# Four query tiles as one Strassen-like set, and a new order of the attention's fillers

## Chip, cores and metric

One core of one Trainium2 chip runs the whole layer. The metric is the device time of the program in microseconds, the median of several runs. All inputs are float32. The engines' short names are those of the profile: PE (TensorE), PEld (its weight loads), DVE (VectorE), ACT (ScalarE), POOL (GpSimd), SP (SyncE, which issues most loads).

## The reference

One decoder layer on 512 tokens of 1024 features. The normalised input `h` goes through one wide projection; the part that matters here is the local branch, with 16 query heads of 64 on 4 key heads:

```python
proj = h @ w_in[i]
qk_ml, v_ml, o_ml, if_pre, q_sw, k_sw, v_sw, g_a, g_b = jnp.split(proj, split_idx, axis=-1)
...
y_b = swa_with_sinks(q_sw.reshape(B, S, SW_Q_HEADS, SW_HEAD_DIM), k_sw..., v_sw..., sinks[i])
merged = jax.nn.sigmoid(g_a) * (y_a @ w_branch_a[i]) + jax.nn.sigmoid(g_b) * (y_b @ w_branch_b[i])
```

Attention is causal with a window of 128 tokens, so a block of 128 queries sees its own and the previous block of keys. The other branch is a chunkwise mLSTM; its queries and keys (`qk_ml`) pass a short convolution and a SiLU. Behind both come the gates, an output projection, an MLP, a gated embedding and a last norm.

## The kernel before

**Products.** Every float32 matrix is split into a high part (a cast on ACT, `wh`) and a low part (a subtraction on DVE, `wl`), and a product is three matmuls per block of 128: high by high, low by high, high by low. `load_w` (L242) makes the parts, four buffers of each deep. `proj_T` (L552) computes one tile, 128 output features for all 512 tokens, in 24 matmuls of 512 columns.

**Sets of seven.** `seven` (L646) multiplies a 2x2 block matrix by another with seven half products instead of eight. One factor is `h`, halved by tokens and by parity of its feature blocks; its parts A11, A12, A22 and its sums S1 to S4 are formed once and kept. The other is a weight in four quarters b11 to b22, which DVE sums in place (four sums of 128x1024). Three PSUM accumulators are used: X (tag `a`, one tile over two banks), Y (tag `t`) and Z (tag `g`). In order: p1 = A11 b11 on X, c11 from A12 b21 on Y, u2 on X with S2, p5 = S1 b11 on Z, c22 with S3 b12 on X, c12 with S4 b22 on Z, c21 with A22 b21 on X. `post` copies p1, u2 and p5 out on ACT and adds them to c11, c12 and c22 on DVE.

`gate_proj` (L837) uses this for the two gate projections: per call two sets of four tiles, each product 24 matmuls of 256 columns (two tiles by four feature blocks by three). Its weights come by `quads` (L264), four loads of 512 KB on SP's queue.

**Queries.** `q_proj` (L617) computes one of eight query tiles with `proj_T` and splits each of its two head halves: ACT casts 64 rows (`qs`), DVE subtracts the rest into the other 64. Tile 0 is made early, tiles 1 to 3 behind the gate projections (L896), tiles 4 to 7 as fillers.

**Attention.** 16 units (two key pairs, four blocks of 128 tokens, two heads). `swa_probs` (L921) is the first part of a unit: eight matmuls (kk, kl), the mask, the maximum, the exponentials on ACT with their sums, the scaling. It runs two units ahead (LOOK). After every fourth unit `swa_out` transposes the probabilities of two blocks and multiplies them by the values (half-array matmuls into `pst`, whose results are `yb`). The key pair 0 reads query tiles 0 to 3, the pair 1 tiles 4 to 7. Ahead of some units one **filler** is called, a projection that the attention doesn't wait for: query tiles 4 to 7 and seven of the eight mLSTM query and key tiles (`qk_proj`, with four more operations for the convolution, `acc`). The eighth stands behind the attention. Eleven slots have a filler:

```python
fill = [lambda: qk_proj(0)] + [lambda i=i: q_proj(i) for i in range(4, 8)]
fill += [lambda i=i: qk_proj(i) for i in (4, 1, 5, 2, 6, 3)]
for u in range(16):
    if u % 3 or u < 3:
        fill.pop(0)()
```

**Order.** Outside the first stage the order on each engine is worked out ahead of time by the framework, from the data's dependences, the buffers and the order of the text as priority; on the chip each engine then runs its instructions in that fixed order. All instructions are issued by one helper, so the trace shows L109 for nearly all of them, and rows are told apart by tiles: `psg<-h,wh` is a filler's or query tile's matmul (`proj_T`), `psa<-hS,wh` and `psg<-hS,wh` are products with the sums of `h`, `psa<-kk,qs` and `psa<-kl,qs` are a unit's logits, `lm` its probabilities.

Of the kernel before, what the change touches and what calls it, by code (L numbers as in the profile page):

```python
# [12 lines left out]
AF = mybir.ActivationFunctionType  # L13
# [104 lines left out]
def block_kernel(  # L118
# [6 lines left out]
    w_o: bass.AP,  # L125
    w_vsif: bass.AP,
    w_qsw: bass.AP,
    w_ksw: bass.AP,
    w_ga: bass.AP,
    w_gb: bass.AP,  # L130
# [51 lines left out]
    def ps_a():  # L182
        return pp.tile([P, 1024], F32, tag="a", bufs=2, name=nm("psa"))
# [9 lines left out]
    def act_r(n="r"):  # L193
        return ap.tile([P, 512], F32R, tag="act", bufs=NACT, name=nm(n))
# [59 lines left out]
    def pairs(a, b):  # L254

        return [(a[0], b[0]), (a[0], b[1]), (a[1], b[0])]
# [295 lines left out]
    def proj_T(wd, i, bank=ps_g):  # L552
        ps = bank()
        mm_T(ps, load_w(wd[i], KT * P, KT), hT)
        return ps
# [58 lines left out]

    qs = {}

    def q_proj(i):  # L617
        ps = proj_T(w_qsw, i)
        for ab in range(2):
            s, o = HALF[ab], HALF[1 - ab]  # L620
            t = act_r("qs")
            A.copy(t[s, :], ps[s, :])
            V.tensor_sub(t[o, :], ps[s, :], r32(t[s, :]))
            qs[i, ab] = t

    q_proj(0)

# [15 lines left out]

    ADDED = {"c11": "p1", "c22": "p5", "c12": "u2"}

    def seven(form, prod, X, Y, Z, b, post, own_first=False, sums_late=False):  # L646

        b11, b12, b21, b22 = b  # L650
        n = range(len(b11))
        for i in n:
            prod(X, A11, form(b11[i]), i, True)
        post("p1", X)

        def weight_sums():
            for i in n:
                V.tensor_sub(b12[i], b22[i], b12[i])
                V.tensor_add(b11[i], b12[i], b11[i])

        if sums_late:
            w21 = [form(t) for t in b21]
            with tc.issue_after(last_low[0].ins):
                weight_sums()
        else:
            weight_sums()
        for i in n:
            prod(Y, A12, w21[i] if sums_late else form(b21[i]), i, True, True)
        own = last_mm[0].ins
        if own_first:  # L670
            with tc.issue_after(last_low[0].ins):
                late_sums()
        post("c11", Y)
        for i in n:
            w = form(b11[i]) if sums_late else None
            with tc.issue_after(last_low[0].ins) if sums_late else ExitStack():
                V.tensor_sub(b21[i], b21[i], b11[i])
            w = w or form(b11[i])
            with tc.issue_after(own) if own_first else ExitStack():
                prod(X, S2, w, i, False)  # L680
            V.tensor_sub(b11[i], b22[i], b11[i])
        post("u2", X)
        for i in n:
            prod(Z, S1, form(b11[i]), i, True)
        post("p5", Z)
        for i in n:
            prod(X, S3, form(b12[i]), i, False)
        post("c22", X)
        for i in n:
            prod(Z, S4, form(b22[i]), i, False, True)  # L690
        post("c12", Z)
        for i in n:
            prod(X, A22, form(b21[i]), i, False, True)
        post("c21", X)


    vm = []
# [124 lines left out]
    def gate_columns():  # L822
# [11 lines left out]
            V.tensor_copy(gc[:, t * NT : t * NT + t + 1, :], pgc[:, t * NT * 4 : (t * NT + t + 1) * 4].rearrange("p (a b) -> p a b", b=4))  # L834
        V.tensor_copy(gc[:, NT * NT :, :], pgc[:, NT * NT * 4 : (NT * NT + NT) * 4].rearrange("p (a b) -> p a b", b=4))

    def gate_proj(wd, beside={}):  # L837

        out_d = [None] * 4
        for j in range(2):  # L840
            raws = quads(wd[4 * j : 4 * j + 4], ["wr"] * 4 if j == 0 else ["pT"] * 2 + ["wr"] * 2)
            X = ps_a().rearrange("p (n c) -> p n c", n=2)[:, :, :256]
            Y, Z = [[new()[:, :256] for _ in range(2)] for new in (ps_t, ps_g)]
            keep = {}
            res = [sp.tile([P, 2, 512], F32, tag="lm", bufs=LMB, name=nm("gr")) for _ in range(2)]

            def prod(ps, f, w, _, first, last=False):
                for t in range(2):
                    ops = []
                    for k in range(4):  # L850
                        ops += pairs([h[:, k, t * P : (t + 1) * P] for h in w], f[k])
                    chain(ps[:, t, :] if ps is X else ps[t], ops, first, last, True)

            def both(op, o, ps, *k):
                if ps is X:
                    op(o, ps, *k)
                else:
                    for t in range(2):
                        op(o[:, t, :], ps[t], *[a[:, t, :] for a in k])

            def post(what, ps):
                if what[0] != "c":
                    keep[what] = act_f(what).rearrange("p (n c) -> p n c", n=2)
                    both(A.copy, keep[what], ps)
                else:
                    half, nh = int(what[1]), int(what[2]) - 1
                    o = res[nh][:, :, 256:] if half == 1 else res[nh][:, :, :256]
                    if what in ADDED:
                        k = keep[ADDED[what]]
                        both(V.tensor_add, k, ps, k)  # L870
                        ps = k
                    A.activation(o, ps, AF.Sigmoid)
                for work in beside.pop((j, what), ()):
                    work()

            seven(lambda r: load_w(None, 1024, 4, r), prod, X, Y, Z, [raws[i : i + 1] for i in range(4)], post)
            for nh in range(2):
                d = dp.tile([P, 2, 512], F32, name=nm("gd"))
                nc.gpsimd.dma_start(out=d, in_=res[nh])
                out_d[2 * nh + j] = d  # L880
        return out_d

    loaded = {}

# [4 lines left out]
            nc.sync.dma_start(out=loaded[0], in_=put[i // 2])  # L889
        return loaded[0][:, i % 2, :]  # L890

    gbd = gate_proj(w_gb, {(0, "p5"): [gates], (1, "c11"): [gate_columns]})
    gad = gate_proj(w_ga)

    for i in range(1, 4):
        q_proj(i)  # L896


    qk = [None] * 8
# [106 lines left out]
    for n in (3, 2, 1):  # L1006
        V.tensor_sub(vd[n], vs[n], vs[n - 1])

    fill = [lambda: qk_proj(0)] + [lambda i=i: q_proj(i) for i in range(4, 8)]
    fill += [lambda i=i: qk_proj(i) for i in (4, 1, 5, 2, 6, 3)]  # L1010
    for u in range(LOOK):
        swa_probs(*units[u])
    for u in range(16):
        if u % 3 or u < 3:
            fill.pop(0)()
        if u + LOOK < 16:
            swa_probs(*units[u + LOOK])
        if u % 4 == 3:
            kp, n, _ = units[u]
            swa_out(kp, (n - 1, n))  # L1020
# [915 lines left out]


_ORDER = [
    "x", "p", "w_qkml", "w_vml", "w_o", "w_vsif", "w_qsw", "w_ksw", "w_ga", "w_gb", "w_a", "w_b", "w_out",
    "w_up", "w_upb", "w_down", "w_pg", "w_pp", "pw", "g_mix", "g_ml", "g_mlp", "g_ple", "g_fin", "conv", "b_if", "sinks",  # L1940
]

# [15 lines left out]
def _halves(w):  # L1958


    return w.reshape(4, 2, P, 2, 2, 256).transpose(4, 1, 3, 2, 0, 5).reshape(8, P, 1024)


def _by_set(w):
# [25 lines left out]
def _layout(i):  # L1990
    w = i["w_in"][0]
    down = i["w_down"][0]
    return {
        "x": i["x"][0],
        "p": i["p"][0, 0].T.reshape(2, P, S).transpose(1, 0, 2).reshape(P, 2 * S),
        "w_qkml": _t_form(w[:, 0:1024]),
        "w_vml": _by_quarter(w[:, 1024:2048]),
        "w_o": _by_quarter(w[:, 2048:3072]),
        "w_vsif": _tok_form(np.concatenate([w[:, 4360:4616], w[:, 3072:3080]], axis=1), KT, 264)[0],
        "w_qsw": _t_form(_heads(w[:, 3080:4104])),  # L2000
        "w_ksw": _t_form(w[:, 4104:4360]),
        "w_ga": _halves(w[:, 4616:5640]),
        "w_gb": _halves(w[:, 5640:6664]),
        "w_a": _t_form(i["w_branch_a"][0]),
        "w_b": _t_form(_heads(i["w_branch_b"][0].T).T),
        "w_out": _by_quarter(i["w_out"][0]),
        "w_up": _t_form(i["w_up"][0][:, :1024]),
        "w_upb": _by_set(i["w_up"][0][:, 1024:]),
        "w_down": np.concatenate([_quarters(down[q * 1024 : (q + 1) * 1024]) for q in range(4)], axis=0),
        "w_pg": _tok_form(i["w_ple_gate"][0], 2, 512),  # L2010
        "w_pp": _tok_form(i["w_ple_proj"][0], 2, 512),
        "pw": np.stack([np.concatenate([i["p"][0, 0].T[o : o + P], i["w_ple_proj"][0][o : o + P, :512]], axis=1) for o in (0, P)]),
        "g_mix": i["norm_mix_g"],
        "g_ml": _columns(i["mlstm_norm_g"][0]),
        "g_mlp": _columns(i["norm_mlp_g"][0]),
        "g_ple": _columns(i["norm_ple_g"][0]),
        "g_fin": i["final_norm_g"][None, :],
        "conv": i["conv_qk"][0].reshape(4, KT, P).transpose(2, 1, 0).reshape(P, KT * 4),
        "b_if": i["b_if"],
        "sinks": i["sinks"],  # L2020
    }
# [19 lines left out]
```

## Time and profile before

| | us |
|---|---|
| median of 3 runs | 862.68 (861.21 to 863.85) |
| the profiled execution | 861.12 |
| its span, first to last instruction | 858.9 |
| PE busy | 849.8 (99%) |
| DVE busy | 712.8 (83%) |
| ACT busy | 526.0 (61%) |
| POOL busy | 59.4 (7%) |

The profiled execution is 2.2 us longer than its span, and 1.56 us shorter than the median. The span falls into the stage of `h` and the first projections (to 122 us), the gate projections (to 204), three query tiles (to 221), the attention (to some 326), the mLSTM and the merge (to 443), and the output projection, the MLP and the rest. PE runs at a granted clock of 0.998 on average. Matmul records overlap one another, and their ends are modelled: the time from one start to the next is the pitch, which the chain of work that ended last shows best, as its pieces lie end to end.

### The profile page before, as it was taken

To read this page: it belongs to the slowest core of one execution; us is meant where nothing else is said; L and a number is where in the kernel's file an instruction comes from. 1 tells how busy PE (TensorE), PEld (TensorE's weight loads), DVE (VectorE), ACT (ScalarE), POOL (GpSimd) and SP (SyncE) were. 2 spreads that over 40 slices of the span, in tenths; PEclk is the share of its full clock that TensorE was granted. 3 is DMA by queue.
4 is the path that set the end of the run, shared out by engine and by line. 5 is a ranking of instruction groups with operands and counts; after the bars stand their busy time and mean duration, and the time that the engine had idled before them with its cause. 6 is when DMAs were issued, how large, how long until landed. Compare 5 with 4: busy or idle time off the path is not lost.

```text
span 858.9 us, 12796 instructions
## 1 busy us (share of the span) xinstructions
PE 849.8 (99%) x4864; PEld 737.9 (86%) x4864; DVE 712.8 (83%) x1039; ACT 526.0 (61%) x907; POOL 59.4 (7%) x92
## 2 busy tenths in 40 slices
PE   9999999999999999999999999999999999999996
PEld 8888789999877878888888888899889989988886
DVE  6998978774698899767897799879988997899657
ACT  7786657554577677863343586458628744774743
POOL 2221111000000000000020000000000000010000
PEclk9999999999999999999999999999999999999999
DMA  8777235436121256565224381743355364634402
GB/s 291 225 206 263 98 124 202 162 129 220 50 98 36 89 177 239 196 245 189 107 52 131 104 228 47 214 134 121 85 186 147 108 172 135 173 102 130 140 1 98
DMA packets 37535, 125.70 MB, mean 146 GB/s; under 512 B 5213, under 2 KB 5213, under 8 KB 37474
## 3 DMA queue, kind: packets, MB, share of 16 engines
q1 hardware_dynamic: 28146, 95.77, 32.2%
q0 software_dynamic: 9184, 28.85, 13.9%
q8 instruction: 38, 0.62, 0.3%
q14 instruction: 23, 0.19, 0.1%
q10 hardware_dynamic: 144, 0.26, 0.1%
HBM read 106.51 MB, written 11.54 MB: 137 GB/s over the span
## 4 chain that ended last, share of the span: by engine, by line
PE 86%; issue 6%; DVE 4%; ACT 2%; DMA 1%; POOL 0%; POOLq 0%; ACTq 0%; DVEq 0%
PE psp L109 34%; PE psg L109 34%; PE psa L109 13%; PE pst L109 5%; ACT lm L109 1%; DVE wl L109 1%; DMA wo<-in_w_out 1%; ACT wh L109 0%; DMA wh<-in_w_b 0%; DVE wr L109 0%; DVE ya L109 0%; DVE lm L109 0%; DVE mx L109 0%; ACT jk L109 0%; DVE wq L109 0%
## 5 line engine op out<-in xcount | busy, mean ns | idle before, releaser
L109 ACT CAST wh<-wr 128x1024 fp32r<-128x1024 f32 (+1 forms) x148 | 153.7, 1049 | 146.4 <-DVE wr L109 52.2
L109 DVE TENSOR_TENSOR wl<-wr,wh 128x1024 fp32r<-128x1024 f32 (+1 forms) x157 | 189.4, 1213 | 56.5 <-ACT wh L109 49.0
L109 PE MATMUL psp<-x,wh 128*128 128x256 f32 x672 | 121.3, 283 | 0.0
L109 PE MATMUL psp<-wh,uf 128*128 128x512 f32 x336 | 106.3, 390 | 0.0
L109 PEld LDWEIGHTS psp<-x,wh 128*128 128x128 f32 x672 | 105.0, 192 | 0.3
L109 PE MATMUL psp<-x,wl 128*128 128x256 f32 x336 | 95.1, 283 | 0.0
L109 PE MATMUL psg<-h,wh 128*128 128x512 f32 x256 | 80.1, 393 | 0.0
L109 PEld LDWEIGHTS psp<-wh,uf 128*128 128x128 f32 x336 | 63.1, 188 | 14.3 <-issue 1.2
L109 ACT CAST wh<-wd 128x1024 fp32r<-128x1024 f32 x45 | 47.2, 1049 | 33.0 <-PE psp L109 27.8
L109 PE MATMUL psp<-wl,uf 128*128 128x512 f32 x168 | 65.5, 390 | 0.0
L109 PEld LDWEIGHTS psp<-x,wl 128*128 128x128 f32 x336 | 64.5, 192 | 0.0
L109 DVE TENSOR_TENSOR wl<-wd,wh 128x1024 fp32r<-128x1024 f32 x45 | 54.7, 1218 | 3.2 <-ACT wh L109 3.2
L109 PEld LDWEIGHTS psg<-h,wh 128*128 128x128 f32 x256 | 46.9, 188 | 8.9
L109 PE MATMUL psg<-h,wl 128*128 128x512 f32 x128 | 50.0, 391 | 0.0
L109 DVE TENSOR_TENSOR uf<-F,uf 128x512 fp32r<-128x512 f32 (+3 forms) x36 | 35.0, 983 | 6.4 <-ACT uf L109 6.4
L109 PE MATMUL psg<-yb,wh 128*128 128x512 f32 x128 | 40.1, 393 | 0.0
L109 PE MATMUL psg<-x,wh 128*128 128x512 f32 x128 | 39.5, 390 | 0.0
L109 DVE TENSOR_TENSOR wr<-wr,wr 128x1024 f32<-128x1024 f32 x31 | 37.9, 1222 | 1.4 <-DMA wr<-in_w_gb 0.5
L109 PEld LDWEIGHTS psp<-wl,uf 128*128 128x128 f32 x168 | 31.5, 188 | 6.7 <-DVE wl L109 0.3
L109 PE MATMUL psg<-wh,uf 128*128 128x512 f32 x112 | 36.5, 389 | 0.0
L109 ACT CAST uf<-F 128x512 fp32r<-128x512 f32 (+3 forms) x36 | 30.7, 856 | 7.5 <-DVE F L109 7.1
L109 PE MATMUL psg<-ya,wh 128*128 128x512 f32 x112 | 34.8, 391 | 0.0
(348 smaller groups left out, 2033.3 us busy)
## 6 DMA issues: line engine op xcount, KB each, us to landing
wr<-in_w_down SPq DMA_DIRECT2D x16, 512.0 KB, 4.1
wd<-in_w_down SPq DMA_DIRECT2D x16, 512.0 KB, 4.3
wr<-in_w_upb SPq DMA_DIRECT2D x12, 512.0 KB, 4.0
wd<-in_w_upb SPq DMA_DIRECT2D x12, 512.0 KB, 4.4
wr<-in_w_qsw SPq DMA_DIRECT2D x8, 512.0 KB, 4.4
gd<-gr POOLq DMA_DIRECT2D x8, 512.0 KB, 3.3
wr<-in_w_qkml SPq DMA_DIRECT2D x8, 512.0 KB, 3.2
wr<-in_w_b SPq DMA_DIRECT2D x8, 512.0 KB, 3.6
```

The lines of the kernel that those rows point to most:

```text
L109: ins = op(*args, **kw)
```

## The change

Query tiles 1 to 4 are no longer four `q_proj` calls (three behind the gate projections, one filler) but one set of seven half products, `q_set`, behind the gate projections, on the kept S1 to S4. The body of `gate_proj` becomes `by_features`, which both use. In the set of queries the order inside `seven` is **swapped**: the S3 product follows the S2 product on X and is copied out (u3), then S1 on Z gives c22 with u3 added, then c21 on X, and c12 last. A result of the set is 256 tokens of two tiles; `put_q` splits it in pieces of 64x256. The fillers are ten: three query tiles and seven of the mLSTM's, in other slots and another order. The weights of the eight query tiles lie in two arrays now.

```diff
+    def put_q(i, c0, n, ps):
         for ab in range(2):
             s, o = HALF[ab], HALF[1 - ab]
-            t = act_r("qs")
+            if (i, ab) not in qs:
+                qs[i, ab] = act_r("qs")
+            t = qs[i, ab][:, c0 : c0 + n]
             A.copy(t[s, :], ps[s, :])
             V.tensor_sub(t[o, :], ps[s, :], r32(t[s, :]))
-            qs[i, ab] = t
+
+    def q_proj(i):
+        put_q(i, 0, S, proj_T(w_qsw, i - 4 if i else 0))
...
         post("u2", X)
+        if swapped:
+            for i in n:
+                prod(X, S3, form(b12[i]), i, False)
+            post("u3", X)
         for i in n:
             prod(Z, S1, form(b11[i]), i, True)
-        post("p5", Z)
-        for i in n:
-            prod(X, S3, form(b12[i]), i, False)
-        post("c22", X)
-        for i in n:
-            prod(Z, S4, form(b22[i]), i, False, True)
-        post("c12", Z)
-        for i in n:
-            prod(X, A22, form(b21[i]), i, False, True)
-        post("c21", X)
+        if swapped:
+            post("c22", Z)
+        else:
+            post("p5", Z)
+            for i in n:
+                prod(X, S3, form(b12[i]), i, False)
+            post("c22", X)
+        rest = [("c12", Z, S4, b22), ("c21", X, A22, b21)]
+        for what, ps, f, b in rest[::-1] if swapped else rest:
+            for i in n:
+                prod(ps, f, form(b[i]), i, False, True)
+            post(what, ps)
...
+    def q_set():
+
+        def done(half, nh, ps):
+            for t in range(2):
+                put_q(1 + 2 * nh + t, 256 if half == 1 else 0, 256, ps[:, t, :])
+
+        by_features(w_qset, ["wr"] * 4, done, swapped=True)
...
-    for i in range(1, 4):
-        q_proj(i)
+    q_set()
...
-    fill = [lambda: qk_proj(0)] + [lambda i=i: q_proj(i) for i in range(4, 8)]
-    fill += [lambda i=i: qk_proj(i) for i in (4, 1, 5, 2, 6, 3)]
+    fill = [lambda: q_proj(7), lambda: qk_proj(6), lambda: q_proj(6), lambda: q_proj(5), lambda: qk_proj(4), lambda: qk_proj(2), lambda: qk_proj(1), lambda: qk_proj(5), lambda: qk_proj(0), lambda: qk_proj(3)]
...
-        if u % 3 or u < 3:
+        if u in (0, 2, 3, 5, 6, 10, 11, 13, 14, 15):
```

## Rows read from the trace of the kernel before

**Rows 1.** The page, busy time of TensorE (share) and its instructions.

```profile
PE 849.8 (99%) x4864; PEld 737.9 (86%) x4864; DVE 712.8 (83%) x1039; ACT 526.0 (61%) x907; POOL 59.4 (7%) x92
```

**Rows 2.** Windows: stretch, its length, each engine's busy time, clock, DMA share, GB/s.

```profile
164.00:204.40 40.40, 40.40 (x338) 40.40 (x337) 28.88 (x31) 22.60 (x31) 2.67 (x5) 1.00 0.44 157
204.40:220.60 16.20, 16.20 (x73) 13.38 (x73) 6.43 (x7) 5.79 (x9) 0.53 (x1) 1.00 0.58 195
220.60:326.20 105.60, 105.42 (x550) 81.36 (x549) 91.35 (x198) 75.56 (x239) 2.14 (x4) 1.00 0.29 98
```

**Rows 3.** Chain that ended last: start us, us, what, instructions.

```profile
21.52 0.87 PE psa L109 x8
...
161.19 5.76 PE psa L109 x48
166.95 2.88 PE pst L109 x24
...
204.39 16.35 PE psg L109 x72
...
276.53 3.58 PE pst L109 x16
```

**Rows 4.** Groups by form, PE, the attention: form, count, busy us, mean ns, idle.

```profile
L109 PE MATMUL psg<-h,wh 128*128 128x512 f32 x193 | 60.8, 394 | 0.0
L109 PE MATMUL psg<-h,wl 128*128 128x512 f32 x97 | 38.0, 392 | 0.0
L109 PE MATMUL psa<-kk,qs 128*128 128x256 f32 x64 | 16.5, 291 | 0.0
...
L109 PE MATMUL psa<-ident,lm 128*128 128x128 f32 x64 | 8.3, 275 | 0.1
L109 PE MATMUL pst<-lm,vs 128*64 128x512 f32 x32 | 7.9, 592 | 0.0
...
L109 PE MATMUL psg<-yb,wh 128*128 128x512 f32 x8 | 2.6, 405 | 0.0
```

**Rows 5.** Groups by form, DVE, the whole span.

```profile
L109 DVE TENSOR_TENSOR wl<-wr,wh 128x1024 fp32r<-128x1024 f32 x154 | 186.9, 1220 | 56.5 <-ACT wh L109 49.0 <-DMA wh<-in_w_b 5.1 <-PE psp L109 2.2
...
L109 DVE TENSOR_TENSOR qs<-psg,qs 64x512 fp32r<-64x512 f32 x16 | 11.0, 688 | 3.3 <-ACT qs L109 2.9
```

**Rows 6.** Timeline, DVE: start us, us, instruction, idle before and its releaser.

```profile
189.25 0.42 DVE L109 TENSOR_TENSOR p<-pst,p 128x256 f32<-128x256 f32 x1
```

**Rows 7.** The page, DMA issues: count, KB each, us to landing.

```profile
wr<-in_w_qsw SPq DMA_DIRECT2D x8, 512.0 KB, 4.4
```

**Rows 8.** Timeline, PE and ACT, around the copy of u2 in `w_ga`'s second set.

```profile
192.70 0.40 PE L109 MATMUL psg<-hS,wh 128*128 128x256 f32 x2
192.78 1.05 ACT L109 CAST wh<-wr 128x1024 fp32r<-128x1024 f32 x1 [1.25 <-PE psa L109]
193.73 0.58 ACT L109 COPY u<-psa 128x512 f32<-128x512 f32 x1
```

**Rows 9.** Timeline, PE, at the attention's start.

```profile
223.39 0.39 PE L109 MATMUL psg<-h,wh 128*128 128x512 f32 x1
223.66 0.39 PE L109 MATMUL psa<-kk,qs 128*128 128x256 f32 x1
223.89 0.28 PE L109 MATMUL psa<-kl,qs 128*128 128x256 f32 x1
224.00 0.40 PE L109 MATMUL psg<-h,wh 128*128 128x512 f32 x1
```

**Rows 10.** Timeline, output projection: a copy out of the bank that PE goes on with.

```profile
442.75 1.09 ACT L109 COPY q<-psg 128x512 f32<-128x512 f32 x2
...
443.38 0.50 PE L109 MATMUL psg<-wh,mg 128*128 128x512 f32 x1 [0.22 <-ACT q L109]
```

**Rows 11.** Timeline, PE and DVE: first and last instruction of one unit's first part.

```profile
287.28 0.28 PE L109 MATMUL psa<-kk,qs 128*128 128x256 f32 x1
...
295.41 0.69 DVE L109 TENSOR_TENSOR lm<-lm,rc 128x512 f32<-128x512 f32 x1
```

More of the change, by code (lines that the diff above doesn't have):

```diff
@@ L127, in block_kernel @@
     w_qsw: bass.AP,
+    w_qset: bass.AP,
     w_ksw: bass.AP,
@@ L615, in block_kernel @@
     qs = {}
-    def q_proj(i):
-        ps = proj_T(w_qsw, i)
+    def put_q(i, c0, n, ps):
         for ab in range(2):
             s, o = HALF[ab], HALF[1 - ab]
-            t = act_r("qs")
+            if (i, ab) not in qs:
+                qs[i, ab] = act_r("qs")
+            t = qs[i, ab][:, c0 : c0 + n]
             A.copy(t[s, :], ps[s, :])
             V.tensor_sub(t[o, :], ps[s, :], r32(t[s, :]))
-            qs[i, ab] = t
+    def q_proj(i):
+        put_q(i, 0, S, proj_T(w_qsw, i - 4 if i else 0))
     q_proj(0)
@@ L644, in block_kernel, with seven @@
     ADDED = {"c11": "p1", "c22": "p5", "c12": "u2"}
-    def seven(form, prod, X, Y, Z, b, post, own_first=False, sums_late=False):
+    def seven(form, prod, X, Y, Z, b, post, own_first=False, sums_late=False, swapped=False):
         b11, b12, b21, b22 = b
@@ L835, in gate_columns, with by_features, prod, both @@
         V.tensor_copy(gc[:, NT * NT :, :], pgc[:, NT * NT * 4 : (NT * NT + NT) * 4].rearrange("p (a b) -> p a b", b=4))
+    def by_features(blocks, tags, done, beside={}, swapped=False):
+        added = dict(ADDED, c22="u3") if swapped else ADDED
+        raws = quads(blocks, tags)
+        X = ps_a().rearrange("p (n c) -> p n c", n=2)[:, :, :256]
+        Y, Z = [[new()[:, :256] for _ in range(2)] for new in (ps_t, ps_g)]
+        keep = {}
+        def prod(ps, f, w, _, first, last=False):
+            for t in range(2):
+                ops = []
+                for k in range(4):
+                    ops += pairs([h[:, k, t * P : (t + 1) * P] for h in w], f[k])
+                chain(ps[:, t, :] if ps is X else ps[t], ops, first, last, True)
+        def both(op, o, ps, *k):
+            if ps is X:
+                op(o, ps, *k)
+            else:
+                for t in range(2):
+                    op(o[:, t, :], ps[t], *[a[:, t, :] for a in k])
+        def post(what, ps):
+            if what[0] != "c":
+                keep[what] = act_f(what).rearrange("p (n c) -> p n c", n=2)
+                both(A.copy, keep[what], ps)
+            else:
+                if what in added:
+                    k = keep[added[what]]
+                    both(V.tensor_add, k, ps, k)
+                    ps = k
+                done(int(what[1]), int(what[2]) - 1, ps)
+            for work in beside.pop(what, ()):
+                work()
+        seven(lambda r: load_w(None, 1024, 4, r), prod, X, Y, Z, [raws[i : i + 1] for i in range(4)], post, swapped=swapped)
     def gate_proj(wd, beside={}):
@@ L840, in gate_proj @@
         for j in range(2):
[L841 to L844, printed above, removed]
             res = [sp.tile([P, 2, 512], F32, tag="lm", bufs=LMB, name=nm("gr")) for _ in range(2)]
[L847 to L876, printed above, removed]
+            def done(half, nh, ps):
+                A.activation(res[nh][:, :, 256:] if half == 1 else res[nh][:, :, :256], ps, AF.Sigmoid)
+            by_features(wd[4 * j : 4 * j + 4], ["wr"] * 4 if j == 0 else ["pT"] * 2 + ["wr"] * 2, done, beside.get(j, {}))
             for nh in range(2):
@@ L881, in gate_proj, with done @@
         return out_d
+    def q_set():
+        def done(half, nh, ps):
+            for t in range(2):
+                put_q(1 + 2 * nh + t, 256 if half == 1 else 0, 256, ps[:, t, :])
+        by_features(w_qset, ["wr"] * 4, done, swapped=True)
     loaded = {}
@@ L890, in gate_of @@
         return loaded[0][:, i % 2, :]
-    gbd = gate_proj(w_gb, {(0, "p5"): [gates], (1, "c11"): [gate_columns]})
+    gbd = gate_proj(w_gb, {0: {"p5": [gates]}, 1: {"c11": [gate_columns]}})
     gad = gate_proj(w_ga)
-    for i in range(1, 4):
-        q_proj(i)
+    q_set()
     qk = [None] * 8
@@ L1938 @@
 _ORDER = [
-    "x", "p", "w_qkml", "w_vml", "w_o", "w_vsif", "w_qsw", "w_ksw", "w_ga", "w_gb", "w_a", "w_b", "w_out",
+    "x", "p", "w_qkml", "w_vml", "w_o", "w_vsif", "w_qsw", "w_qset", "w_ksw", "w_ga", "w_gb", "w_a", "w_b", "w_out",
     "w_up", "w_upb", "w_down", "w_pg", "w_pp", "pw", "g_mix", "g_ml", "g_mlp", "g_ple", "g_fin", "conv", "b_if", "sinks",
@@ L1961, in _halves, with _one_set @@
     return w.reshape(4, 2, P, 2, 2, 256).transpose(4, 1, 3, 2, 0, 5).reshape(8, P, 1024)
+def _one_set(w):
+    return w.reshape(4, 2, P, 2, 256).transpose(1, 3, 2, 0, 4).reshape(4, P, 1024)
 def _by_set(w):
@@ L1992, in _layout @@
     down = i["w_down"][0]
+    q_sw = _heads(w[:, 3080:4104])
     return {
@@ L1999, in _layout @@
         "w_vsif": _tok_form(np.concatenate([w[:, 4360:4616], w[:, 3072:3080]], axis=1), KT, 264)[0],
-        "w_qsw": _t_form(_heads(w[:, 3080:4104])),
+        "w_qsw": np.concatenate([_t_form(q_sw[:, :P]), _t_form(q_sw[:, 5 * P :])], axis=0),
+        "w_qset": _one_set(q_sw[:, P : 5 * P]),
         "w_ksw": _t_form(w[:, 4104:4360]),
```

## The prediction

> **What bounds the kernel now.** I read the page first. TensorE (PE) is busy for 99% of the span [rows 1]. A reader should not stop there: matmul records overlap and their ends are modelled, so a busy PE can still be waiting. The second view, busy time by stretch, has to say where another engine could be behind it [rows 2]. In the gate stage (164.0 to 204.4 us) PE and its weight loads fill everything while VectorE (DVE) has 28.88 of 40.40 us. In the three query tiles behind it DVE has 6.43 of 16.20. In the attention (220.6 to 326.2) it has 91.35 of 105.60, so there it is close behind PE. The clock column stands at 1.00 in all of them, the upper level of 2.4 GHz; the change leaves no gap long enough to give a reason for another level.
>
> The third view, the chain that ended last, gives the pitch of the matmuls, because its pieces lie end to end [rows 3]. A product of 24 matmuls with 256 columns takes 2.88 us, 120 ns each. Seventy-two with 512 columns take 16.35 us, 227 ns each, so one query tile (24 of them) costs 5.45 us. Eight transposes take 0.87 us, 109 ns each. Sixteen half-array products take 3.58 us, 224 ns each.
>
> With these pitches I add up the attention's PE work from its counts [rows 4]: 193 + 97 filler matmuls at 227 ns are 65.8 us; 64 kk and as many kl at 120 ns, 15.4; 64 transposes, 7.0; 56 half-array products (32 of lm, the others of pT), 12.5; and 12 first matmuls of the next stage, 2.7. That is 103.4 us in a stretch of 105.6. So **PE is the bound in the attention too**, and only some 2.2 us are waits, in pieces of about a tenth of a microsecond. A change here earns what it takes from PE's work, and loses what it adds in waits.
>
> **The change, part by part.**
>
> *Query tiles one to four.* Removed: 4 x 5.45 = 21.80 us of PE. Added: seven products of the gate stage's kind, 7 x 2.88 = 20.16 us. **PE saves 1.64 us.** The work also moves: before, three tiles (16.35 us) stood ahead of the attention and four were fillers; now 20.16 us stand ahead of it and three are fillers. The attention thus starts 3.8 us later and holds 5.45 us less PE work.
>
> The Trainium skill, page "TensorE: Matmul & The Clock Gate", section "Back-to-back issue gap", gives 262 cycles for 256 columns and 518 for 512. At 2.4 GHz that would be an estimate of 109 and 216 ns, and a saving of 2.4 us instead of 1.64. The chain's pieces show 120 and 227 ns, so I keep 1.64.
>
> *DVE.* Removed for four tiles: a low part of 1.22 us and two query subtractions of 0.69 us each [rows 5], 4 x 2.60 = 10.4 us. Added: seven low parts and four weight sums, 11 x 1.22 = 13.4 us; three additions in two pieces of 128x256 at 0.42 [rows 6], 2.5 us; sixteen subtractions of 64x256. Such a subtraction is not in the trace. Half of the 64x512 one would be 0.34, the 128x256 addition is 0.42; I take 0.42, the row with the same number of columns, 6.7 us. Together 22.7, **12.3 us more on DVE**. It is paid at nothing for the most part: DVE has 11.5 + 9.8 us idle in the two stretches ahead of the attention [rows 2], and the low parts are made some products ahead. What spills is the last post (two additions, four subtractions, 2.5 us). The attention's DVE work becomes 91.35 - 2.6 + 2.5 = 91.2 us in about 100.2, a share of 0.91 where it was 0.87. The cover gets thinner; it is not gone. ScalarE gains three more casts (3 x 1.05) and smaller copies, in stretches where it has 18 us idle of 40 [rows 2]; I cost that at nothing.
>
> *Loads.* Four 512 KB loads in the place of four; half a megabyte lands in 4.4 us [rows 7]. The last two wait on SP's queue for buffers that the second gate pass gives back, as the second gate projection's loads wait for the first's. At that seam the chain runs without a break: the 48 matmuls from 161.19, two products with the seam between them, take 5.76 us, and the next product 2.88 [rows 3]. Only later weight loads queue behind them on SP. Nothing.
>
> *The swapped order.* Here a wait is added. Before, the S1 product stood between the S2 and the S3 product on bank X, and hid the copy of u2. Now S3 follows S2 on X and must wait for that copy. What is queued behind it is all of PE. The second gate projection shows the copy's time: the next product begins at 192.70, the copy of u2 starts at 193.73, behind a weight cast on ScalarE, and takes 0.58 [rows 8]. If PE stood still until then, it would lose 194.31 - 192.70 = 1.6 us. That is the upper bound. The lower is a switch between products: where the order slips single kk, kl pairs between filler matmuls, the pitch from kk to kl is 0.23 instead of 0.12 us [rows 9], 0.1 for a switch and 0.2 for there and back. The order is worked out ahead by the framework from its own estimates, and these rows show that it fills a foreseen wait with other ready matmuls; the S1 product is ready there. Where nothing else was allowed, in the output projection, PE did stand: its next matmul was let go by the copy q at 443.38, idle for 0.22 us in the record [rows 10]. I take **+0.4**, near the filling rows. The later swap (c21 ahead of c12) has one product between every copy and its reuse, so nothing there.
>
> The Trainium skill, "Perfetto Trace Analysis", section "Optimizing Tensor Performance" (Matmuls), advises rotating independent matmul groups through different banks, so that one's evacuation overlaps the next one's matmuls. S3 right behind S2 on X breaks that rule. What it costs by the rows is the 1.6 us above, and that is the second rival below.
>
> *The attention's start.* c21 completes the queries for the first two blocks one product ahead of the end. Before, the first unit's last pairs waited for the third tile and went out singly at 223.66, 3 us after the last query matmul [rows 9]. Now they can go at once. That gives the units' chain a lead, and PE nothing directly.
>
> *Slots.* Ten fillers in place of eleven, and three empty slots in a row (7, 8, 9) where no two were adjacent. A unit's own PE work is (15.4 + 7.0 + 12.5) / 16 = 2.2 us. Its chain runs from its first kk at 287.28 to the scaled probabilities at 296.10 (295.41 + 0.69) [rows 11], of which PE's pairs take the first 1.0; that leaves 7.8 us, or 3.9 per unit with two in flight. So a unit without a filler leaves PE up to 1.7 us short, unless a filler is drawn forward; nothing in the data forbids that, as queries and keys need only h. Bounds: 1.5 us better (most of the 2.2 us of waits go with the earlier start), 5.1 worse (three slots short). I take **+0.3**, for the thinner cover on DVE.
>
> *Sum.* -1.64 + 0.4 + 0.3 = **-0.9 us**. Behind the attention nothing is touched, and PE bounds it too, so the end moves with it. The profiled execution took 861.12 us (span 858.9, and 2.2 around it) and would take 860.2. The median of the runs shown is 1.56 above it, so the forecast as a median is **861.7**.
>
> **The rivals.**
> 1. *The waits go as well.* The lead at the start and the slots put near the end (13, 14, 15) take 1.5 of the attention's 2.2 us, and the switch costs 0.2: -1.64 + 0.2 - 1.5 = -2.9, **859.7** as a median. For it: the waits are there, and the start's pairs are seen to wait. Against: DVE's share rises to 0.91.
> 2. *S3 waits for u2 in full.* The order keeps S3 in place, or the copy comes later than foreseen, behind the cast: -1.64 + 1.6 + 0.3 = +0.3, **863.0**. The change then saves no time although it saves work. For it: the cast ahead of the copy in the gate stage. Against: the order's filling elsewhere.
> 3. *The empty slots starve PE* (the slower side). Fillers stay in their slots, and between the fillers of slots 6 and 10 PE waits for the units' chain. The filler of slot 6 covers one slot, the others lack 1.7 each: 3.4 to 5.1, I take 4.2. -1.64 + 0.4 + 4.2 = +3.0, **865.7**. It decides once less than about one filler is drawn forward into these slots. For it: DVE at 0.91, a chain of 3.9 against 2.2 of PE work. Against: before, fillers are seen cut up and spread between the units.
>
> **How the numbers follow.** Chances: forecast 0.45, rival one 0.17, two 0.18, three 0.20. About 0.3% (2.6 us) is what a measurement of this kernel can tell from no change. The forecast's own range is 860.5 to 863.7, inside that bound; rival two lies inside as well, one beyond it on the fast side, and three beyond it on the slow side unless its price is at the lower end. So: faster 0.19, same 0.63, slower 0.18. The range for 8 in 10 takes in the first rival and most of the third: 858.8 to 866.0. The saving is small beside the waits it could add, which is why "no difference" leads although I expect a gain.
>
> **What would show it right or wrong.** After: the gate stage's pitch of 2.88 goes on for seven more products, and the attention begins about 4 us later but ends about 1 us earlier. PE's matmuls at the S2, S3 seam change bank within a product (filled) or stop for over 1 us (rival two). In the attention the windows' DVE share is near 0.9; kk and kl in blocks of eight at its start; if rival three holds, PE's idle time between the second third's units shows releasers on DVE or ScalarE. The forecast is wrong if the half products run slower than 120 ns, if the seam from gate to queries waits for a load, or if the stage behind the attention gains waits that it did not have.

## The result and the profile after

| | before | after |
|---|---|---|
| median of 22 runs each, us | 862.36 (861.21 to 863.85) | 863.93 (862.48 to 866.34) |
| ratio to before, 95% interval | | 1.0019 (1.0013 to 1.0026) |
| the profiled execution, us | 861.12 | 864.31 |
| its span, us | 858.9 | 862.5 |

The change costs 1.57 us. That is inside the 0.3% which the prediction called no change, and inside its range. But it has the other sign than the -0.9 us forecast, and the interval leaves out equality. So some 2.5 us are to be explained.

The page of after, its busy row (columns as in [rows 1]):

```profile
PE 849.2 (98%) x4936; PEld 739.7 (86%) x4936; DVE 722.8 (84%) x1060; ACT 532.5 (62%) x921; POOL 59.3 (7%) x92
```

Windows of after for the stretches of [rows 2]: the set of queries with what precedes it, and the attention (stretch, its length, busy time of PE, PEld, DVE, ACT, POOL, granted clock, DMA share, GB/s):

```profile
206.20:226.50 20.30, 20.30 (x167) 19.90 (x165) 15.34 (x22) 12.23 (x20) 0.53 (x1) 1.00 0.60 208
226.50:329.80 103.30, 100.19 (x525) 76.91 (x525) 88.81 (x202) 73.07 (x239) 2.13 (x4) 1.00 0.31 104
```

PE now has 3.1 us idle in the attention, where [rows 2] shows 0.2. DVE's share there is 0.86, no higher than before, though DVE does 10 us more in the whole span. So a larger share of DVE in the attention is not where the loss comes from.

The chain that ended last, with a point ahead of the first changed instruction and one behind the attention, first of before and then of after (start, us, what, instructions):

```profile
125.49 2.88 PE pst L109 x24
...
369.40 0.72 PE pst L109 x6
```

```profile
126.91 2.88 PE pst L109 x24
...
200.04 2.88 PE psg L109 x24
202.92 5.17 PE psa L109 x44
...
301.74 6.97 DMA wh<-in_w_b
...
311.55 5.49 PE psg L109 x23
...
372.93 0.72 PE pst L109 x6
```

The two profiled executions differ by 1.42 us before anything has changed (125.49 against 126.91); a difference of spans would count that in. From point to point it is 243.91 us before and 246.02 after, +2.11. The set has 1.64 us less PE work in that stretch, so waits have grown by 3.75. Following PE's starts in the timeline, I find them in three places: 0.42 at the swapped seam, 1.01 ahead of 242.85 and 2.31 ahead of 311.55, together 3.74. Small waits elsewhere about balance.

**The seam.** S3 adds to what S2 left on X, so it may not start before the copy of u2 has read X. Timeline of after, ACT and PE, where S1 (on `psg`) fills that wait, S3 (on `psa`) follows, and later c21 (`psa<-h,wh`) follows the copy of u3 (start, us, instruction):

```profile
215.31 0.58 ACT L109 COPY u<-psa 128x512 f32<-128x512 f32 x1
215.72 0.28 PE L109 MATMUL psg<-hS,wh 128*128 128x256 f32 x1
215.94 0.51 PE L109 MATMUL psa<-hS,wh 128*128 128x256 f32 x2
...
219.95 0.58 ACT L109 COPY u<-psa 128x512 f32<-128x512 f32 x1
220.59 0.51 PE L109 MATMUL psa<-h,wh 128*128 128x256 f32 x2
```

Thirteen of S1's matmuls stand ahead of S3 and eleven behind it. S3 starts at 215.94, just as the copy of u2 ends (215.89), and the pitch is 0.22 us instead of 0.12 right ahead of its first matmul and right behind it. The same happens at 220.59, where c21 starts just as the copy of u3 ends (220.53): the eleven matmuls left of S1 and one pair of logits do not quite cover that copy. Four such pitches make the 0.42 us, half of it at S3 and half at c21.

**The start.** Timeline of after, DVE and ACT, from the end of the c21 product (223.57) on; a bracket gives the idle time ahead and its releaser:

```profile
224.60 0.36 ACT L109 CAST qs<-psa 64x256 fp32r<-64x256 f32 x1
...
226.19 0.42 DVE L109 TENSOR_TENSOR qs<-psa,qs 64x256 fp32r<-64x256 f32 x1
...
226.65 0.37 ACT L109 CAST qs<-psa 64x256 fp32r<-64x256 f32 x1 [1.68 <-DVE qs L109]
...
231.95 1.29 DVE L109 TENSOR_TENSOR lm<-psa,later_key 128x512 f32<-128x512 f32 x2
...
235.50 1.28 ACT L109 ACT_TABLE_LOAD   x1
236.79 0.21 ACT L109 ACTIVATE es<-ds 128x4 f32<-128x4 f32 x1
...
242.06 1.35 DVE L109 COPY_PREDICATED lm<-later_key,psa 128x512 f32<-128x512 int32 x2
```

The posts of c21 read X in turns, a cast on ACT and then a subtraction on DVE, with weight parts of 1.05 and 1.23 us between them. The fourth cast starts at 230.08, 6.5 us after the product, and the first mask at 231.95. The exponentials then wait for a table load of 1.28 us. Before, that load ran beside the first mask, and nothing waited for it: the first exponential behind it waited for DVE. Timeline of before, DVE and ACT:

```profile
224.21 0.69 DVE L109 TENSOR_TENSOR lm<-psa,later_key 128x512 f32<-128x512 f32 x1 [0.60 <-PE psa L109]
224.24 1.28 ACT L109 ACT_TABLE_LOAD   x1
227.16 0.40 ACT L109 ACTIVATE lm<-lm,nmx 128x128 f32<-128x128 f32 x1 [1.64 <-DVE nmx L109]
```

In after, PE comes to a standstill where its next logits need the bank that the first of the two COPY_PREDICATED of 242.06 still reads:

```profile
241.61 0.39 PE L109 MATMUL psg<-h,wl 128*128 128x512 f32 x1
242.85 0.38 PE L109 MATMUL psa<-kk,qs 128*128 128x256 f32 x1 [0.85 <-DVE lm L109]
```

**The end of the attention.** Timeline of after, POOL, DVE and PE:

```profile
301.74 0.53 POOL L249 DMA_DIRECT2D wh<-in_w_b  x1 [93.65 <-PE psg L109]
...
305.46 0.73 DVE L109 SCALAR_TENSOR_TENSOR acc<-psg,cw,acc 128x511 f32<-128x511 f32 x1
306.11 0.15 DVE L109 SCALAR_TENSOR_TENSOR nmx<-mx,nsink 128x4 f32<-128x4 f32 x1
308.73 1.23 DVE L109 TENSOR_TENSOR wl<-wr,wh 128x1024 fp32r<-128x1024 f32 x1 [2.48 <-DMA wh<-in_w_b]
309.88 0.74 DVE L109 SCALAR_TENSOR_TENSOR acc<-psg,cw,acc 128x510 f32<-128x510 f32 x1
...
310.65 0.75 DVE L109 SCALAR_TENSOR_TENSOR acc<-psg,cw,acc 128x509 f32<-128x509 f32 x1
...
311.55 0.70 PE L109 MATMUL psg<-h,wh 128*128 128x512 f32 x2 [2.14 <-DVE sm L109]
```

Read it from the end. PE starts its next projection at 311.55, right behind `acc` (310.65 + 0.75), the last of the convolution's operations that read the old result out of a `psg` bank. (The bracket names `sm`, a short instruction of DVE that comes next behind `acc`.) Two `acc` stand behind `wl`, a low part of the next stage's first weight, the first tile of `branch_b`, and DVE stands still for 2.48 us because that weight is still landing. For this stage POOL's queue loads the high part itself, with a cast on the way (`cast=True`), and the load took 6.97 us from issue to landing. In the kernel before, the load was issued at 294.22 and landed in 4.9 us, and the same low part started at 301.62 without a wait, with the last `acc` of the projection then finished ahead of it (timeline, POOL and DVE):

```profile
294.22 0.54 POOL L248 DMA_DIRECT2D wh<-in_w_b  x1 [87.55 <-PE psg L109]
...
298.54 0.74 DVE L109 SCALAR_TENSOR_TENSOR acc<-psg,cw,acc 128x509 f32<-128x509 f32 x1
...
301.62 1.21 DVE L109 TENSOR_TENSOR wl<-wr,wh 128x1024 fp32r<-128x1024 f32 x1
```

Less the 1.42 us by which the two executions differ from the start, the load is now issued 6.1 us later, while the attention's end moved by 2.2 (326.2 to 329.8, less 1.42). The load waits for a filler's matmul that frees its buffer, and the fillers stand in other slots.

### The profile page after: what moved, and what is told of

Read it like the earlier page. It is cut to its first block, busy times and chain, and to the rows that moved or that the text cites. A ratio compares the mean times of both kernels' runs of the same rounds, so it can differ in the third digit from the quotient of the medians.

```text
span 862.5 us, 12974 instructions
## 1 busy us (share of the span) xinstructions
PE 849.2 (98%) x4936; PEld 739.7 (86%) x4936; DVE 722.8 (84%) x1060; ACT 532.5 (62%) x921; POOL 59.3 (7%) x92
## 4 chain that ended last, share of the span: by engine, by line
PE 73%; issue 16%; DVE 6%; DMA 3%; ACT 1%; SPq 0%; POOL 0%; POOLq 0%; DVEq 0%; ACTq 0%
PE psp L109 34%; PE psg L109 27%; PE psa L109 10%; PE pst L109 2%; DVE wl L109 2%; DMA wh<-in_w_b 1%; DVE wr L109 1%; DMA wq<-in_w_vml 1%; DMA xt<-in_x 1%; DMA wr<-in_w_qsw 1%; DVE s L109 0%; DVE wq L109 0%; DVE kl L109 0%; ACT wh L109 0%; DVE xn L109 0%
## 5 line engine op out<-in xcount | busy, mean ns | idle before, releaser
L109 ACT CAST wh<-wr 128x1024 fp32r<-128x1024 f32 (+1 forms) x151 | 156.7, 1049 | 144.8 <-DVE wr L109 52.8
L109 DVE TENSOR_TENSOR wl<-wr,wh 128x1024 fp32r<-128x1024 f32 (+1 forms) x160 | 192.7, 1213 | 50.9 <-ACT wh L109 43.4
L109 PE MATMUL psg<-h,wh 128*128 128x512 f32 x192 | 60.5, 394 | 2.1 <-DVE sm L109 2.1
L109 DVE TENSOR_TENSOR wr<-wr,wr 128x1024 f32<-128x1024 f32 x35 | 42.7, 1221 | 2.0 <-DMA wr<-in_w_gb 0.7
L109 PEld LDWEIGHTS psg<-h,wh 128*128 128x128 f32 x192 | 35.2, 188 | 10.6 <-ACT es L109 2.4
L109 PE MATMUL psg<-h,wl 128*128 128x512 f32 x96 | 37.8, 393 | 0.0
```

The costliest lines, as they stand in the source:

```text
L109: ins = op(*args, **kw)
```

## The experiments

Ratios are to the kernel before, measured in the same series, with 95% intervals; its median was 862.26 in the first four, 862.29 in the next four and 862.36 in the last four and in the result's own. The theories go by letters in the quoted texts: W is the wait for `branch_b`'s first load in DVE's queue, S the new order and slots by themselves, P the set with its posts, and C the chain of posts at the attention's start.

### 1. Which part of the change costs the time

**act_cast1**: the first tile of `branch_b` gets its high part by a cast on ACT, so that its load is an ordinary one.

```diff
-        mm_T(ps, load_w(w_b[i], KT * P, KT, cast=True), yb)
+        mm_T(ps, load_w(w_b[i], KT * P, KT, cast=i > 0), yb)
```

> The changed kernel, but the first tile of the next stage (branch_b(0)) takes its high part by a cast on ScalarE, not by a casting transfer on POOL's queue; TensorE's order stays the same. Theory W (the loss is single waits): TensorE's 2.3 us wait at 311.55 goes, as its cause, VectorE standing 2.48 us behind the low part wl for a load that landed late, is gone: about 2 us under the changed kernel's 863.93, so 861.5 to 862.3. Theory F (VectorE is too full in the attention, and any wait taken away comes back elsewhere): less than 0.6 us won, 863.3 or more.

Measured: 861.74 us, 0.9993 (0.9984 to 1.0001), against 1.0019 for after. Timeline, DVE and PE, at the place of the 2.3 us wait:

```profile
302.89 1.22 DVE L109 TENSOR_TENSOR wl<-wr,wh 128x1024 fp32r<-128x1024 f32 x1
...
308.30 0.71 PE L109 MATMUL psg<-h,wh 128*128 128x512 f32 x2
```

Neither waits any more, and 2.2 us are back. The wait of 1.0 us at the start stays (at 241.98). So W is the largest part of the loss.

**set_old_fill**: the set of queries with the old order of fillers, without tile 4, slot 1 left empty.

```diff
+    fill = [lambda: qk_proj(0)] + [lambda i=i: q_proj(i) for i in range(5, 8)]
+    fill += [lambda i=i: qk_proj(i) for i in (4, 1, 5, 2, 6, 3)]
...
-        if u in (0, 2, 3, 5, 6, 10, 11, 13, 14, 15):
+        if u != 1 and (u % 3 or u < 3):
```

> The set of seven for the queries alone: the fillers stay in the old order and slots without tile 4 (slot 1 empty). Theory S (the new slots cost the time, the set earns its 1.64 us less about 0.4 at the swapped seam): 861.0 to 861.8. Theory P (the set itself costs, as its last results are posted late, the attention starts late and has a filler less): 863 to 865.

Measured: 865.18 us (5 runs), 1.0038 (1.0026 to 1.0050), slower than after and a little above theory P's range. The 2.3 us wait is absent, but three others take its place, of 0.83, 0.82 and 1.56 us over the pitch. The longest, in the timelines of DVE and PE:

```profile
262.58 1.23 DVE L109 TENSOR_TENSOR wl<-wr,wh 128x1024 fp32r<-128x1024 f32 x1
263.84 1.41 DVE L109 TENSOR_TENSOR qs<-psg,qs 64x512 fp32r<-64x512 f32 x2
...
264.59 0.73 PE L109 MATMUL psg<-h,wh 128*128 128x512 f32 x2 [1.40 <-DVE qs L109]
```

Again a bank's last reader on DVE (`qs<-psg`) stands behind a low part, though here one that waits for no load. So the set without its new slots loses more; the slots repair some of that and bring the wait of 2.3 us. With the seam these waits make 3.63 us, less 1.64 about +2.0; the ratio says +3.3 (2.2 to 4.3). Smaller waits, of 0.42 us ahead of 298.68 and of some 0.2 ahead of 225.50, 229.97 and 249.44, add 1.1.

**slots_alone**: the kernel before with the new order and slots, tile 4 as an eleventh filler in slot 1.

```diff
+    fill = [lambda: q_proj(4), lambda: q_proj(7), lambda: qk_proj(6), lambda: q_proj(6), lambda: q_proj(5), lambda: qk_proj(4), lambda: qk_proj(2), lambda: qk_proj(1), lambda: qk_proj(5), lambda: qk_proj(0), lambda: qk_proj(3)]
...
+        if u in (0, 1, 2, 3, 5, 6, 10, 11, 13, 14, 15):
```

> The kernel before with the new order and slots of the fillers, tile 4 as an eleventh in slot 1; no set. Theory S (the slots cost): 863.5 to 865. Theory P (the set costs): 861.8 to 862.9, as before.

Measured: 862.48 us, 1.0005 (0.9996 to 1.0013). S falls. It is also the cleanest contrast to after. The load is late here too (6.3 us from issue to landing), but the last reader of the bank stands ahead of the low part in DVE's queue, and PE goes on:

```profile
305.72 0.74 DVE L109 SCALAR_TENSOR_TENSOR acc<-psg,cw,acc 128x509 f32<-128x509 f32 x1
...
307.69 1.23 DVE L109 TENSOR_TENSOR wl<-wr,wh 128x1024 fp32r<-128x1024 f32 x1 [1.16 <-DMA wh<-in_w_b]
```

**unswapped**: the set in the order of the gate projections.

```diff
-        by_features(w_qset, ["wr"] * 4, done, swapped=True)
+        by_features(w_qset, ["wr"] * 4, done)
```

> The changed kernel with the order inside the seven as in the gate projections (S1 between S2 and S3, c12 ahead of c21). If the swap earns its place by giving the first two blocks' queries one product earlier, this is 1 to 3 us slower than the changed kernel: 865 to 867. If the swap's seam (S3 waits for the copy of u2, 0.2 to 0.4 us in the trace) costs more than it gives, it is 0.2 to 1 us faster: 862.9 to 863.7.

Measured: 863.82 us, 1.0027 (1.0016 to 1.0038); the interval holds after's 1.0019, and the time lies in neither range. The swap neither gains nor costs anything clear of the noise: without it the four small waits at the seam are gone, and one of 1.2 us stands at the start of the attention, where PE waits for the last queries' posts:

```profile
229.32 0.39 PE L109 MATMUL psa<-kk,qs 128*128 128x256 f32 x1 [1.04 <-DVE qs L109]
```

### 2. The control, and the wait at the start

**before_cast1**: the edit of act_cast1 in the kernel before.

> The kernel before, with the same edit as act_cast1 (the first tile of branch_b casts on ScalarE). Control. If the cast is worth something by itself, this falls by 1 us or more under 862.3. Theory W (the transfer hurts only where the order puts the low part ahead of the bank's last reader, as in the changed kernel): TensorE does not wait for it here, so 861.8 to 862.8.

Measured: 862.19 us, 0.9992 (0.9981 to 1.0003). Where DVE doesn't wait for the load, the edit brings nothing that can be told from zero. So the 2.2 us of act_cast1 are a loss undone, not a gain of another kind, as far as some 1 us of noise can tell.

**cast1_table**: act_cast1, and an exponential of one column in the posts of c11, which brings the table load forward.

```diff
         def done(half, nh, ps):
+            if half == 1 and nh == 0:
+                A.activation(small("ex", 1, 1), ps[:, 0, :1], AF.Exp, scale=0.0)
```

> act_cast1, and one exponential of a single column right behind c11 of the query set, so that ScalarE loads the exponential's table there, where it is idle, and not ahead of the first unit (1.28 us at 235.50). Theory C (the attention's start is a chain behind the set's last posts, and TensorE's 1.0 us wait at 242.85 is its end): 0.7 to 1.3 us under act_cast1's 861.74, so about 860.7. Theory D (VectorE's work in the start sets it): 861.5 to 862.

Measured: 861.01 us, 0.9983 (0.9973 to 0.9994), 0.7 us under act_cast1. The two intervals overlap, so the times alone would not settle it; the trace does. The table is loaded ahead of the attention (timeline, ACT), and the wait of 1.0 us is gone; one of 0.42 at 257.15 is new, which leaves some 0.6.

```profile
210.40 1.28 ACT L109 ACT_TABLE_LOAD   x1
```

**cast1_banks**: act_cast1, and the posts ordered by head halves, meant to let ACT cast from one bank while DVE subtracts from the other.

```diff
-            for t in range(2):
-                put_q(1 + 2 * nh + t, 256 if half == 1 else 0, 256, ps[:, t, :])
+            for ab in range(2):
+                for t in range(2):
+                    put_q(1 + 2 * nh + t, 256 if half == 1 else 0, 256, ps[:, t, :], (ab,))
```

> act_cast1, and the pieces of a result posted head half by head half, so that consecutive casts and subtractions read different banks (in the changed kernel ScalarE's second cast of c21 waits 1.68 us for VectorE's subtraction on the same bank). Theory C: the queries for the first unit come some 2 us earlier, and the 1.0 us wait at 242.85 shrinks by half or more: 861.0 to 861.4. Theory D: as act_cast1, 861.5 to 862.

Measured: 861.37 us, 0.9985 (0.9975 to 0.9995). The time is in theory C's range, the mechanism only in part. The two engines still take turns: the second cast waits 1.47 us for DVE, where act_cast1 has 1.69 (timeline, ACT):

```profile
225.23 0.37 ACT L109 CAST qs<-psa 64x256 fp32r<-64x256 f32 x1 [1.47 <-DVE qs L109]
```

The first mask starts 7.9 us behind the end of the c21 product (222.36 to 230.21) instead of 8.4, and the small waits of 0.2 us near 226 and 230 shrink to 0.1 or less. The wait of 1.0 us stays (at 241.32). It thus hangs on the table load, not on the posts alone.

**cast1_both**: both edits.

> act_cast1 with both edits, the early table and the posting by head halves. Theory C: the 1.0 us wait is gone and part of the small ones at the start: 860.3 to 860.9. Theory D: 861.4 or more.

Measured: 860.75 us, 0.9979 (0.9969 to 0.9990). Windows of this kernel over the places of the two larger waits, where PE has 0.96 and 2.14 us idle in after:

```profile
226.00:246.00 20.00, 20.00 (x105) 16.86 (x105) 17.54 (x41) 14.60 (x48) 0.00 (x0) 1.00 0.24 84
300.00:316.00 16.00, 16.00 (x84) 13.52 (x83) 14.63 (x30) 9.20 (x29) 1.07 (x2) 1.00 0.51 164
```

### 3. Late load or queue order, the price of the seam, the empty slots

**after_order**: act_cast1 took away the casting load and the wait together. Here the load stays as it is, and DVE's low part of the first tile is held behind the convolution of query and key tile 0.

```diff
-            V.scalar_tensor_tensor(
+            conv_end[i] = V.scalar_tensor_tensor(
...
-        mm_T(ps, load_w(w_b[i], KT * P, KT, cast=True), yb)
+        with tc.issue_after(conv_end[0].ins) if i == 0 else ExitStack():
+            w = load_w(w_b[i], KT * P, KT, cast=True)
+        mm_T(ps, w, yb)
```

> The changed kernel with the casting transfer kept, but VectorE's low part of the first tile of branch_b held behind the convolution of the query and key tile 0, the bank's last reader. Theory W (the loss was VectorE's queue: a low part that waits for a landing load stood ahead of the reader that frees TensorE's bank): the 2.3 us wait goes without the cast, 861.5 to 862.3. Theory L (the late load itself sets the time, as branch_b needs it): 863.3 or more.

Measured: 861.59 us, 0.9991 (0.9982 to 1.0000), the same as act_cast1. Timeline, DVE: the `acc` go first, and the low part behind them waits for nothing. The load itself is no faster: 7.3 us from issue (301.52) to landing.

```profile
308.88 2.31 DVE L109 SCALAR_TENSOR_TENSOR acc<-psg,cw,acc 128x511 f32<-128x511 f32 x3
311.11 2.35 DVE L109 TENSOR_TENSOR wl<-wr,wh 128x1024 fp32r<-128x1024 f32 x2
```

So the late load alone costs nothing here; what cost 2.3 us is the place of the low part that waits for it in DVE's fixed order.

**order_both**: after_order with the table and bank edits.

> The early table, the posting by head halves and the low part held behind the convolution, with the transfer kept instead of the cast on ScalarE. If the three waits are all there was, this is as fast as cast1_both: 860.4 to 861.1. If the late load costs later on: 861.5 or more.

Measured: 860.66 us, 0.9979 (0.9970 to 0.9987), as cast1_both. The two ways of removing the wait are worth the same.

**seam_forced**: after, with the S1 product held behind the last S3 matmul, so that nothing fills the wait for u2.

```diff
+            s3_end = last_mm[0].ins
...
-            prod(Z, S1, form(b11[i]), i, True)
+            with tc.issue_after(s3_end) if swapped else ExitStack():
+                prod(Z, S1, form(b11[i]), i, True)
```

> The changed kernel with the S1 product of the query set held behind the last S3 matmul, so that nothing fills TensorE's wait for the copy of u2. Theory of the prediction's second rival: a single wait of 0.8 to 1.6 us at the seam in place of the four small ones of 0.1 us, and 0.4 to 1.2 us more than the changed kernel: 864.3 to 865.1. If the copy's wait is absorbed by the attention's start (which waits for VectorE anyhow): 863.5 to 864.2.

Measured: 864.66 us (5 runs), 1.0033 (1.0020 to 1.0047), 0.7 us above after. The intervals overlap, so the trace has to show it. Timeline, PE and ACT: one wait, 1.42 us over the pitch, and the copy of u2 stands behind a weight cast, as the prediction's second rival has it.

```profile
213.09 1.04 ACT L109 CAST wh<-wr 128x1024 fp32r<-128x1024 f32 x1 [1.02 <-PE psa L109]
214.04 0.58 ACT L109 COPY u<-psa 128x512 f32<-128x512 f32 x1
...
214.68 0.50 PE L109 MATMUL psa<-hS,wh 128*128 128x256 f32 x2 [1.26 <-ACT u L109]
```

With all 24 matmuls of S1 behind S3, c21 no longer waits for the copy of u3. The large wait at the end of the attention is 1.92 us here instead of 2.31, so not all of what the seam adds (1.1 us) shows in the time.

**both_slot8**: cast1_both, with the filler of slot 10 in slot 8.

```diff
-        if u in (0, 2, 3, 5, 6, 10, 11, 13, 14, 15):
+        if u in (0, 2, 3, 5, 6, 8, 11, 13, 14, 15):
```

> cast1_both with the filler of slot 10 called in slot 8, so that no three slots in a row are empty. The prediction's third rival (empty slots starve TensorE): 859.8 or less, a gain of 1 us or more. If the order spreads the fillers over the units anyway: as cast1_both, 860.3 to 861.3.

Measured: 860.49 us, 0.9978 (0.9968 to 0.9987), as cast1_both. Three empty slots in a row cost nothing that can be seen.

## Why the prediction was off

**Right.**
- The set saves 1.64 us of PE work. In the timeline of after, c11 starts at 208.51 and c12 at 223.57, five products later; less the seam's 0.42 us and a pair of logits (0.24) that leaves 14.40, 2.88 for each product. So the half products are no slower than in the gate stage, and the loads on SP hold up nothing. With the two larger waits removed, three kernels (cast1_both, order_both, both_slot8) stand at 0.9978 and 0.9979, 1.8 to 1.9 us under before, and under after as well. The seam's 0.42 is still in them, and -1.64 + 0.42 = -1.2 lies in their intervals (0.9969 to 0.9990 is -2.7 to -0.9 us). What their edits of the start would do in the kernel before was not run; there nothing waits for the table load.
- A 64x256 subtraction at 0.42: it measures 0.42. DVE's total grew by 10.0 rather than 12.3 us, with the counts as forecast. The durations of the changed operations, added singly, grew by 12.1; the busy time counts ends that overlap only once.
- Rival three (empty slots) does not hold, by both_slot8. Rival one does not either: the waits grew.

**Right by luck in part.**
- The swapped seam: +0.4 taken, 0.42 seen. The fill by S1 was the right reason, and taking it away made a wait of 1.42 where the upper bound was 1.6; rival two had the right price for a case that did not come. But only 0.2 of the 0.42 stands at S3. The other 0.2 stands at c21, of which the prediction says *"one product between every copy and its reuse, so nothing there"*: the thirteen matmuls that filled the first gap were missing from the cover of the second.

**Wrong.**
- *"That gives the units' chain a lead, and PE nothing directly."* This step looked at when c21's product ends and not at what stands between it and the first logits: casts and subtractions in turns, weight parts between them, and a table load on ACT which was hidden before and now stands between the first unit's mask and its exponentials. The first mask comes 8.4 us after the product's end (223.57 to 231.95). The step was costed at nothing and measured 1.0 us (PE's wait ahead of 242.85, gone with the earlier table load, some 0.6 of it net), with some tenths from the posts: cast1_both, with both edits, is 1.0 us under act_cast1 (860.75 against 861.74). kk and kl in blocks of eight, named as a sign of the lead, come only from 231.13; the first pairs go out singly at 220.24 and 226.67.

  The Trainium skill, "ScalarE: Activation LUTs", section "What ACT_TABLE_LOAD costs", gives the load 1283 ns and adds a drain of some 1380 for a switch to another set. The trace agrees with the load, 1.28 us, and shows no such drain: the cast ahead ends at 235.48, the load starts at 235.50, and the next ACTIVATE starts at 236.79.
- *Slots, +0.3*, with *"behind the attention nothing is touched"*. With the set and the new order together, the end of the attention has a wait of 2.3 us, and its cause is the first load of the stage behind it. The bounds of this term (-1.5 to +5.1) hold it, but by another mechanism than the one they were worked out for. I weighed DVE's share, 0.91 forecast and 0.86 measured, and the share says nothing about order. What the step lacked is a question to each in-order queue: which instruction waits for a load, and which reader of a PSUM bank stands behind it? The first weight of the stage behind the attention is loaded and split inside the attention, into a buffer that a filler frees, so the slots move that stage's start as well.
- *The sum itself* adds the set and the slots as if each had a price of its own. Against before, the slots alone stand at 1.0005, the set with the old slots at 1.0038, and both together at 1.0019. So the slots cost nothing clear of the noise by themselves, and they make the set cheaper; the 2.3 us belong to neither alone. slots_alone has the late load without the bad order, set_old_fill has no late load but other bad orders.
- *"the change leaves no gap long enough to give a reason for another level"* of the clock. The change left PE idle for 2.14 us. In after's profiled execution the granted clock behind it stayed at 1.00; the last section shows one execution of unswapped in which it did not.

Two things stay open. Why the framework put the low part ahead of the two `acc` is not shown; a landing time in its estimate shorter than the 6.97 us measured would do it. And what made the load take 6.97 us was not tried. A pair of other loads (`vl`) was in flight from 300.23 on. In the six kernels where that pair was issued within 3.5 us ahead of this load, it took 6.3 to 7.5 us (after, unswapped, seam_forced, after_order, order_both, slots_alone); in before and set_old_fill, where the pair came 9 us behind it, 4.9 and 3.6. That fits a load slowed by the pair, and does not prove it.

## What to carry to other kernels

An engine's share of busy time does not tell whether its queue will hold another engine up. Where the order is fixed ahead, look in each queue for instructions that wait for a load, and for readers of a PSUM bank behind them; one such pair cost 2.3 us here, more than the whole saving. When work is moved, ask also which buffers the next stage's first loads need, and where a one-off such as a table load now falls. And parts of a change that share a queue have no prices to be added: each of the two here cost something else alone than with the other.

## What the runs showed of the hardware

A wait can cost more than its length; one execution shows it. In unswapped's profiled execution, one of its longest at 866.57 us, PE stood idle for 2.49 us at the place of the large wait, and the granted clock of the next 4.4 us was 0.61 on average: eight matmuls came 427 ns apart instead of 227, at the lower of the two levels (1.2 and 2.4 GHz), some 1.6 us lost. After, idle for 2.14 us at the same place, kept 1.00. Two cases give no rule. Windows of unswapped, then of after:

```profile
311.60:316.00 4.40, 4.40 (x13) 3.46 (x14) 4.40 (x7) 0.30 (x1) 0.00 (x0) 0.61 0.30 108
```

```profile
311.60:316.00 4.40, 4.40 (x20) 3.63 (x21) 4.40 (x7) 0.29 (x1) 0.00 (x0) 1.00 0.36 117
```

The three longest runs of after (865.20, 865.58 and 866.34) have a mean granted clock of 0.995 to 0.996 where the others have 0.997 to 0.999. That would fit a fall of this kind in some executions; those runs have no trace to show it.

The table load's price was hidden until it fell on a path that mattered: 1.28 us on ACT made 1.0 us on PE, and an exponential of one column, issued 16 us ahead of the attention, took that wait off, with one of 0.42 us new behind it.
